# Seven-product units in the second half of the down-projections of a two-layer encoder, and wide turns at the borders

## The chip, the cores and the metric

One core of one Trainium2 chip. The metric is the device time of one execution in microseconds (us), the median of several runs; times inside it come from one profiled execution. Five engines run beside each other: TensorE (PE: matmuls, and PEld: loads of their weights), VectorE (DVE), ScalarE (ACT), GpSimd (POOL) and SyncE (SP, which issues most of the DMAs).

## The reference

A trunk of two encoder layers over 256 positions of width 2048, in float32. Layer 0 mixes tokens with grouped-query attention, layer 1 with dilated sliding-window attention. Behind each mixer stands a gated MLP:

```python
def conv_ffn(h, w_up, conv_w, conv_b, w_down):
    u = h @ w_up                                   # 2048 -> 2 * 5632
    u = depthwise_conv_width_3_over_positions(u, conv_w) + conv_b
    gate, val = jnp.split(u, 2, axis=-1)
    return (jax.nn.silu(gate) * val) @ w_down      # 5632 -> 2048

for i in range(2):
    hn = rms_norm(h, mix_norm[i])
    h = h + (mixer_a(hn, ...) if i == 0 else mixer_b(hn, ...))
    h = h + conv_ffn(rms_norm(h, ffn_norm[i]), w_up[i], conv_w[i], conv_b[i], w_down[i])
return rms_norm(h, final_norm)
```

## The kernel before

The 256 positions are two row blocks m of 128, and the residual `h` stays on the chip. A matmul of float32 precision is made of three: each operand is split into a high part (a copy by ACT in a shorter format) and a low part (the difference, by DVE), and high x high, high x low and low x high are added up in PSUM. Weights come in chunks of 512 rows (`kg`, four k-tiles) by 512 columns (`n`), as two raw tiles of 128x1024. `feed` (L106) handles one chunk: it loads the two raw tiles, has ACT make `wh` (L136) and DVE `wl` (L137) from each, and issues 24 matmuls: 4 k-tiles, 2 row blocks, 3 products (L124 to L126). `wh` and `wl` have four buffers each (`NHL`). The splits are issued under `high_priority` with an offset of `AHEAD` = 60: the scheduler may place them up to 60 instructions ahead of other work of their engine.

The MLP (`ffn`) goes through the 5632 hidden columns in two halves of 6 and 5 blocks of 512. In each half the up-projection makes a gate block and a value block in turn; `value_gen`, `gate_gen` and `flush` are generators that turn them, convolve them, multiply them and split the product for the down-projection (`act_split`). `step()` runs one piece of a generator between matmuls: those in `pending` in order, those in `beside` with `step(True)`. Then the half's down-projection adds its chunks into the residual, column block by column block (n = 0 to 3). Each column block has two PSUM accumulators, one for each row block; there are four accumulators (`new_acc`) and four other PSUM tiles (`ps_tile`).

In the first half two of the six chunks, 2 and 3, go through **seven-product units**. For a pair of column blocks, `fast_unit` (L496) treats the chunk as a 2x2 by 2x2 block product (blocks: pairs of k-tiles by row blocks on the left, pairs of k-tiles by column blocks on the right) and does it with 7 block products in place of 8: 42 matmuls in place of 48. It needs four sums of weights by DVE (L513), into the tiles `u`, and seven splits (ACT L514, DVE L515). The sums on the left are made once by `combined` (L479), when the chunk's product is split. Products 2, 4, 3 and 8 go straight into the four accumulators of the two column blocks, products 1, 5, 6 and 7 into the four other PSUM tiles. `fold` (L526) adds those into `h` afterwards: one copy by ACT, eight instructions by DVE. `pair` (L550) runs a list of (chunk, side): side 0 or 1 is a plain feed for one of the two column blocks, side None is a unit. Before the first unit it runs all generators to their end. The first half's list is: chunks 0 and 1 for both sides, unit 2, chunk 4 for both, unit 3, chunk 5 for both. The second half has no unit: `project2` (L193) handles columns 0 and 1 with the last chunk of both kept for the end, `project` columns 2 and 3, each with five chunks. In the last layer `project_last` handles columns 3 and the final norm.

`done` adds an accumulator to `h` (`add_residual`, L340) and, where a column block is final, sums squares (ACT) and starts `late_transpose` (L282). That one turns a quarter of `h` (a column block) for the next up-projection: for n < 3 with 16 block transposes on DVE (`block_T`, L275, recorded at L277), for n = 3 with two wide transposes (`quad_T`, L268) and moves of 32-row blocks on POOL, ACT and DVE. `out_proj` (L720) does the same behind the mixers.

Of the kernel before, what the change touches and what calls it, by code (L numbers as in the profile page):

```python
# [30 lines left out]
def tile_encoder(ctx: ExitStack, tc: tile.TileContext, x, xT, w_a, w_ao, q_gain, k_gain, w_b, w_bo,  # L31
# [249 lines left out]

    def late_transpose(hT, n, g, pool, tag):  # L282
        def put(kt, src):
# [4 lines left out]
        if n < 3:  # L288
            t = pool.tile([P, 4, NT], F32, tag=tag, name=nm("tT"), bufs=1)
            for b in range(4):  # L290
                yield
                for gr in range(4):
                    block_T(t, h[:, :, n * 512:(n + 1) * 512], b, gr)
            yield
            for j in range(4):
                put(4 * n + j, t[:, j, :])
            return
# [73 lines left out]
    def ffn(l, hT, ss_in, cw, g_next, last, side=None):  # L371
        with tc.tile_pool(name=nm("fpool"), bufs=1) as fp:
# [90 lines left out]
            def act_split(value):  # L463
                slots, k0 = value[5:]
                cv = value[2]
                if k0 // 4 in fast:
                    slots[-1 - k0 // 4] = combined(cv, k0)
                    ready.add(k0 // 4)
                    yield
                    return  # L470
                for j in range(4):
                    hi, lo = slots[k0 + j]
                    tc.keep_in_program_order(nc.scalar.activation(hi, cv[:, j, :], AF.Copy))
                    nc.vector.tensor_tensor(lo, cv[:, j, :], hi.bitcast(F32), ALU.subtract)
                    if j == 1:
                        yield
                ready.add(k0 // 4)

            def combined(cv, k0):  # L479
# [12 lines left out]
                for q, i in ((5, 0), (6, 1), (7, 2), (3, 3)):  # L492
                    pick[q] = own[0][:, i], own[1][:, i]
                return pick

# [30 lines left out]
            def fold(acc, n0, n1):  # L526
# [3 lines left out]
                tt = nc.vector.tensor_tensor  # L530
                one, two = (fp.tile([P, 2, 512], F32, tag="quad", name=nm("fold"), bufs=2) for _ in range(2))
                a, v, w, c = one[:, 0], one[:, 1], two[:, 0], two[:, 1]
                nc.scalar.activation(a, acc[1], AF.Copy)
                yield
                tt(v, acc[6], a, ALU.subtract)
                yield
                tt(w, acc[7], v, ALU.add)
# [4 lines left out]
                tt(hs(0, n0), hs(0, n0), a, ALU.add)  # L542
                yield
                tt(hs(1, n0), hs(1, n0), w, ALU.subtract)
                yield
                tt(hs(0, n1), hs(0, n1), c, ALU.add)
                yield
                tt(hs(1, n1), hs(1, n1), v, ALU.add)

            def pair(wd, ns, lhs, order, done, hurry=False):  # L550
                (a3, a8), (a2, a4) = new_acc(), new_acc()
                acc, begun = {2: a2, 3: a3, 4: a4, 8: a8}, set()
                sides = [a2, a4], [a3, a8]
                fasts = [kg for kg, side in order if side is None]
                for i, (kg, side) in enumerate(order):
                    while kg not in ready:
                        step()
                    if side is None:
# [10 lines left out]
                        if kg == fasts[-1]:  # L569
                            beside.append(fold(acc, *ns))  # L570
                        continue
                    mine = ((2, 4), (3, 8))[side]
                    end = not any(s == side for _, s in order[i + 1:])
                    feed(sides[side], lhs, kg, wd[ns[side], kg], not begun.issuperset(mine), end,
# [5 lines left out]
                    if end:  # L580
                        done(sides[side], ns[side])

# [13 lines left out]
            for hf, (p0, p1) in enumerate(HALVES):  # L596
                slots = {}
                ready.clear()
                new_us()
                fast = (2, 3) if hf == 0 else ()  # L600
                last_value = None
# [21 lines left out]
                def done(accs, n):  # L623
# [12 lines left out]
                    if hf == 1:  # L636
                        sumsq_cols(ss, n, junk)
                        start(late_transpose(hTn, n, g_next, fp, "cg"))

# [64 lines left out]
                both = {kg: [(kg, 0), (kg, 1)] for kg in rest}  # L704
                if not fast:
                    done(project2(wd, 0, 1, slots, rest, 1, lambda a: done(a, 0)), 1)
                    for n in (2, 3):
                        if last and n == 3:
                            project_last(wd, n, slots, rest, first_out, last_out)
                        else:  # L710
                            done(project(wd, n, slots, rest), n)
                    continue
                f0, f1 = ([(kg, None)] for kg in fast)
                for ns in (0, 1), (2, 3):
                    pair(wd, ns, slots, both[0] + both[1] + f0 + both[4] + f1 + both[5], done, ns[0] == 0)
            assert not spare
            extra[0] = None
        return hTn, ss

    def out_proj(w, slots, kgs, late, g_next, junk, pool, tag, cuts=()):  # L720
        hTn, ss = {}, new_ss()

        def done(accs, n):
            add_residual(accs, n)
            sumsq_cols(ss, n, junk)
            start(late_transpose(hTn, n, g_next, pool, tag))

# [36 lines left out]
    def mixer_a():  # L764
        with tc.tile_pool(name="apool", bufs=1) as ap:
# [246 lines left out]
            for g in range(4):  # L1012
                start(attend(g, project(w_a, g, hT, kgs)))
            return *out_proj(w_ao, slots, kgs, 1, 1, junk, ap, "t2", (2,)), cw

# [23 lines left out]
    def mixer_b(hT, ss_in):  # L1039
        with tc.tile_pool(name="bpool", bufs=1) as bp:  # L1040
# [29 lines left out]
            for hf in range(2):  # L1070
# [156 lines left out]
                for g in range(3):  # L1227
                    accs = project(w_b, 6 * g + 4 + hf, hT, kgs)
                    vs[g] = evac_split(bp, accs, rstd, v12[:, g - 1] if g else None)
                    if g == 0:  # L1230
                        start(value_stage())
            return *out_proj(w_bo, slots, [0, 2, 4, 1, 3, 5], 3, 3, junk, bp, "vl"), cw

# [88 lines left out]
```

## Time and profile before

| | |
|---|---|
| median of 3 runs | 2249.04 us (2248.47 to 2250.51) |
| profiled execution | 2247.76 us, of which the span from first to last instruction is 2246.0 us |
| busy: PE, PEld | 2233.1 us, 1852.2 us |
| busy: DVE, ACT, POOL | 1686.5 us, 1259.0 us, 733.0 us |
| granted TensorE clock, mean over the span | 0.999 |

A matmul's recorded duration (0.39 us) is longer than the distance between two of them, since they are pipelined. What a piece of work costs PE is therefore read from stretches of time and the number of matmuls in them, not from the sum of durations. An engine's busy share over the span is a mean over stages that have different limits.

### The profile page before, as it was taken

How to read it: one execution, taken by the hardware profiler on the slowest of the kernel's cores; microseconds unless marked ns; L12 is line 12 of the kernel's file. 1: busy time of each engine (PE TensorE's matmuls, PEld its weight loads, DVE VectorE, ACT ScalarE, POOL GpSimd, SP SyncE). 2: the span in 40 equal slices, each digit the busy share in tenths (PEclk: the TensorE clock that was granted, in tenths of full speed). 3: DMA queues.
4: the chain of work that ended last, by engine and by line, in shares of the span. 5: the costliest groups of instructions: out<-in, count | busy, mean ns of one | idle time of the engine just before them, and what ended most of it. 6: DMA issues, size and time to landing. Idle time of an engine off the chain costs nothing.

```text
span 2246.0 us, 28619 instructions
## 1 busy us (share of the span) xinstructions
PE 2233.1 (99%) x10041; PEld 1852.2 (82%) x10041; DVE 1686.5 (75%) x2241; ACT 1259.0 (56%) x1747; POOL 733.0 (33%) x971
## 2 busy tenths in 40 slices
PE   9999999999999999999999999999999999999998
PEld 7888888888888888888888888888888888888887
DVE  6877967778876776878886877686777798676765
ACT  7675555666545656555454554445655655465653
POOL 2342055662006553010052007002756500256510
PEclk9999999999999999999999999999999999999999
DMA  8665666665665566565556555566656566666663
GB/s 303 192 215 186 210 192 200 190 194 188 198 207 194 192 195 193 189 196 195 186 192 193 179 188 174 179 203 210 193 186 201 187 205 204 189 196 194 209 196 132
DMA packets 126048, 439.56 MB, mean 196 GB/s; under 512 B 14280, under 2 KB 18120, under 8 KB 125904
## 3 DMA queue, kind: packets, MB, share of 16 engines
q1 hardware_dynamic: 123056, 429.05, 59.1%
q0 software_dynamic: 2560, 8.39, 1.5%
q8 instruction: 78, 1.28, 0.2%
q14 instruction: 66, 0.54, 0.1%
q10 hardware_dynamic: 288, 0.30, 0.0%
HBM read 432.34 MB, written 5.34 MB: 195 GB/s over the span
## 4 chain that ended last, share of the span: by engine, by line
PE 93%; DVE 3%; POOL 2%; issue 1%; ACT 1%; DMA 1%; SPq 0%; DVEq 0%; POOLq 0%; ACTq 0%
PE acc L125 29%; PE acc L126 29%; PE acc L124 29%; POOL wide L272 2%; PE ps L521 1%; DMA raw<-in_w_a_dram 1%; PE ps L522 1%; DVE wl L515 1%; PE ps L520 1%; DVE wl L137 1%; PE acc L521 0%; PE acc L522 0%; PE acc L520 0%; PE ps L234 0%; PE ps L233 0%
## 5 line engine op out<-in xcount | busy, mean ns | idle before, releaser
L137 DVE TENSOR_TENSOR wl<-raw,wh 128x1024 fp32r<-128x1024 f32 (+1 forms) x772 | 961.7, 1250 | 419.6 <-ACT wh L136 413.9
L136 ACT ACTIVATE wh<-raw 128x1024 fp32r<-128x1024 f32 (+1 forms) x772 | 807.8, 1050 | 721.4 <-PE acc L126 645.8
L124 PE MATMUL acc<-wh,xh 128*128 128x512 f32 x2176 | 848.8, 390 | 0.2 <-ACT wh L136 0.2
L125 PE MATMUL acc<-wl,xh 128*128 128x512 f32 x2176 | 848.1, 390 | 0.5 <-DVE wl L137 0.4
L126 PE MATMUL acc<-wh,xh 128*128 128x512 f32 x2176 | 847.7, 390 | 0.0
L432 POOL COPY u<-quad 32x256 f32<-32x256 f32 x672 | 473.3, 704 | 349.0 <-DVE quad L268 322.6
L125 PEld LDWEIGHTS acc<-wl,xh 128*128 128x128 f32 x2176 | 409.0, 188 | 85.0 <-DVE wl L137 2.0
L124 PEld LDWEIGHTS acc<-wh,xh 128*128 128x128 f32 x2176 | 409.3, 188 | 84.3 <-ACT wh L136 0.6
L126 PEld LDWEIGHTS acc<-wh,xh 128*128 128x128 f32 x2176 | 408.9, 188 | 84.8
L124 PE MATMUL acc<-wh,a 128*128 128x512 f32 x880 | 343.0, 390 | 0.0
L125 PE MATMUL acc<-wl,a 128*128 128x512 f32 x880 | 342.5, 389 | 0.0
L126 PE MATMUL acc<-wh,a 128*128 128x512 f32 x880 | 342.5, 389 | 0.0
L126 PEld LDWEIGHTS acc<-wh,a 128*128 128x128 f32 x880 | 165.1, 188 | 34.5 <-DVE a L219 0.2
L125 PEld LDWEIGHTS acc<-wl,a 128*128 128x128 f32 x880 | 165.2, 188 | 33.9
L124 PEld LDWEIGHTS acc<-wh,a 128*128 128x128 f32 x880 | 165.3, 188 | 33.8
L272 POOL COPY wide<-quad 32x256 f32<-32x256 f32 x165 | 107.2, 650 | 171.8 <-DVE quad L268 162.7
L402 POOL MEMSET u<- 128x4 f32 x12 | 1.0, 105 | 400.0 <-DVE wl L515 212.2
L368 ACT ACTIVATE stg<-acc,rstd 128x512 f32<-128x512 f32 x122 | 82.8, 684 | 32.8 <-PE acc L126 32.8
L449 POOL TENSOR_TENSOR cv<-cg,cv 128x1024 f32<-128x1024 f32 x18 | 58.2, 3233 | 108.9 <-DVE cv L419 103.6
L419 DVE SCALAR_TENSOR_TENSOR cg<-u,cw,cg 128x256 f32<-128x256 f32 x176 | 82.2, 510 | 4.5 <-ACT cg L411 4.5
L419 DVE SCALAR_TENSOR_TENSOR cv<-u,cw,cv 128x256 f32<-128x256 f32 x176 | 73.6, 477 | 2.8 <-ACT cv L411 2.8
L268 DVE STREAM_TRANSPOSE quad<-stg 128x512 f32<-128x512 f32 x88 | 59.0, 696 | 8.6 <-ACT stg L368 8.6
(219 smaller groups left out, 1514.7 us busy)
## 6 DMA issues: line engine op xcount, KB each, us to landing
raw<-in_w_up_dram SPq DMA_DIRECT2D x352, 512.0 KB, 4.6
raw<-in_w_down_dram SPq DMA_DIRECT2D x176, 512.0 KB, 4.5
raw<-in_w_b_dram SPq DMA_DIRECT2D x144, 512.0 KB, 4.4
raw<-in_w_bo_dram SPq DMA_DIRECT2D x48, 512.0 KB, 3.9
raw<-in_w_a_dram SPq DMA_DIRECT2D x40, 512.0 KB, 4.7
raw<-in_w_ao_dram SPq DMA_DIRECT2D x32, 512.0 KB, 4.2
raw<-in_w_a_dram SPq DMA_DIRECT2D x16, 256.0 KB, 5.7
there<-quad POOLq DMA_DIRECT2D x6, 512.0 KB, 3.3
```

The costliest lines, as they stand in the source:

```text
L124: nc.tensor.matmul(accs[m], xh, wh[:, j, :], start=st, stop=False)
L125: nc.tensor.matmul(accs[m], xh, wl[:, j, :], start=False, stop=False)
L126: nc.tensor.matmul(accs[m], xl, wh[:, j, :], start=False, stop=sp)
L136: nc.scalar.activation(wh[:, c], r[:, c], AF.Copy)
L137: nc.vector.tensor_tensor(wl[:, c], r[:, c], wh[:, c].bitcast(F32), ALU.subtract)
L268: nc.vector.transpose(quad[:, :, at, :], src.rearrange("p (x c t) -> p c x t", c=4, t=32))
L272: nc.gpsimd.tensor_copy(o[32 * c:32 * c + 32, :, 32 * q:32 * q + 32], quad[32 * q:32 * q + 32, c])
L368: nc.scalar.activation(o[:, m, :], accs[m], AF.Copy, scale=rstd[:, m:m + 1])
L419: nc.vector.scalar_tensor_tensor(cj, halves(flat[:, j, o:o + NT])[:, ::-1], tap(n, j, i), cj, ALU.mult, ALU.add)
L432: nc.gpsimd.tensor_copy(o, src)
L449: made.append(eng.tensor_tensor(cv, cg, cv, ALU.mult).ins)
L515: nc.vector.tensor_tensor(wl, r, wh.bitcast(F32), ALU.subtract)
```

## The change

1. The units of the first half handle chunks 1 and 2 in place of 2 and 3 (`fast = (1, 2)` in both halves), and the list becomes: chunks 0 and 3, unit 1, chunk 4, unit 2, chunk 5.
2. In the second half columns 0 and 1 go through `pair` with two units: chunks 0 and 3 for both sides, unit 1, chunk 4 for side 0, unit 2, chunk 4 for side 1. Columns 2 and 3 stay plain. So chunks 1 and 2 are kept in both forms: `combined` hands back its parts, and `plain_too` makes the one split that the plain form lacks (into a slot of its own) and records the plain k-tiles.
3. `pair` takes its accumulators in another order (those of side 0 first), a side ends where no later feed or unit adds to it, and in the second half `finish` runs the fold to its end before `done`.
4. `fold` uses the tiles `stg` and `st` and yields less often.
5. `late_transpose` turns the quarters n < 3 with two wide transposes and 16 block moves, in turn on POOL and ACT, four to a step; callers hand in the tile for it.

```diff
@@ -279,21 +279,32 @@
 
     next_space = [None]
 
-    def late_transpose(hT, n, g, pool, tag):
+    def quad_place(o, quad, i0, i1):
+        for i in range(i0, i1):
+            q, c = QC[i]
+            dst, src = o[32 * c:32 * c + 32, :, 32 * q:32 * q + 32], quad[32 * q:32 * q + 32, c]
+            if i % 2:
+                nc.scalar.activation(dst, src, AF.Copy)
+            else:
+                nc.gpsimd.tensor_copy(dst, src)
+
+    def late_transpose(hT, n, g, pool, tag, new_quad):
         def put(kt, src):
             hT[kt] = new_hT(kt)
             split_scaled(*hT[kt][:2], src, gain[:, g, kt:kt + 1])
 
         yield
         if n < 3:
-            t = pool.tile([P, 4, NT], F32, tag=tag, name=nm("tT"), bufs=1)
-            for b in range(4):
-                yield
-                for gr in range(4):
-                    block_T(t, h[:, :, n * 512:(n + 1) * 512], b, gr)
+            quad = new_quad()
+            for m in range(2):
+                quad_T(quad, slice(m, 8, 2), h[:, m, n * 512:(n + 1) * 512])
             yield
+            o = wide_tile(pool, tag)
+            for i in range(0, 16, 4):
+                quad_place(o, quad, i, i + 4)
+                yield
             for j in range(4):
-                put(4 * n + j, t[:, j, :])
+                put(4 * n + j, o[:, 2 * j:2 * j + 2].rearrange("p m c -> p (m c)"))
             return
         space, quad_tag, wide_tag = next_space[0]
         src = h[:, :, n * 512:(n + 1) * 512]
@@ -464,7 +475,9 @@
                 slots, k0 = value[5:]
                 cv = value[2]
                 if k0 // 4 in fast:
-                    slots[-1 - k0 // 4] = combined(cv, k0)
+                    slots[-1 - k0 // 4], *parts = combined(cv, k0)
+                    if hf == 1:
+                        plain_too(k0, 20 + 2 * fast.index(k0 // 4), *parts)
                     ready.add(k0 // 4)
                     yield
                     return
@@ -491,7 +504,15 @@
                 pick = {1: (hA[:, 0], lA[:, 0]), 2: (hA[:, 1], lA[:, 1]), 4: (hB, lB)}
                 for q, i in ((5, 0), (6, 1), (7, 2), (3, 3)):
                     pick[q] = own[0][:, i], own[1][:, i]
-                return pick
+                return pick, v, sx
+
+            def plain_too(k0, spot, v, sx):
+                c = pair_slot(spot, [P, 2, 2, P], F32R, "c")
+                split_in_order(c[:, 0], c[:, 1], v[:, 0, :, 1])
+                for kt in range(4):
+                    b, j = divmod(kt, 2)
+                    one = (sx[:, 4, j], sx[:, 5, j]) if b else (c[:, 0, j], c[:, 1, j])
+                    slots[k0 + kt] = (sx[:, b, j], one[0]), (sx[:, 2 + b, j], one[1])
 
             def fast_unit(acc, pick, wap0, wap1, begun, end):
                 def load(wap, i):
@@ -528,30 +549,33 @@
                     return h[:, m, n * 512:(n + 1) * 512]
 
                 tt = nc.vector.tensor_tensor
-                one, two = (fp.tile([P, 2, 512], F32, tag="quad", name=nm("fold"), bufs=2) for _ in range(2))
+                one, two = (fp.tile([P, 2, 512], F32, tag=t, name=nm("fold")) for t in ("stg", "st"))
                 a, v, w, c = one[:, 0], one[:, 1], two[:, 0], two[:, 1]
                 nc.scalar.activation(a, acc[1], AF.Copy)
                 yield
                 tt(v, acc[6], a, ALU.subtract)
-                yield
                 tt(w, acc[7], v, ALU.add)
                 yield
                 tt(c, acc[5], v, ALU.add)
                 tt(v, acc[5], w, ALU.add)
                 yield
                 tt(hs(0, n0), hs(0, n0), a, ALU.add)
-                yield
                 tt(hs(1, n0), hs(1, n0), w, ALU.subtract)
                 yield
                 tt(hs(0, n1), hs(0, n1), c, ALU.add)
-                yield
                 tt(hs(1, n1), hs(1, n1), v, ALU.add)
 
             def pair(wd, ns, lhs, order, done, hurry=False):
-                (a3, a8), (a2, a4) = new_acc(), new_acc()
+                (a2, a4), (a3, a8) = new_acc(), new_acc()
                 acc, begun = {2: a2, 3: a3, 4: a4, 8: a8}, set()
                 sides = [a2, a4], [a3, a8]
                 fasts = [kg for kg, side in order if side is None]
+
+                def finish(side):
+                    while beside and hf == 1:
+                        step(True)
+                    done(sides[side], ns[side])
+
                 for i, (kg, side) in enumerate(order):
                     while kg not in ready:
                         step()
@@ -568,9 +592,11 @@
                         fast_unit(acc, lhs[-1 - kg], wd[ns[0], kg], wd[ns[1], kg], begun, end)
                         if kg == fasts[-1]:
                             beside.append(fold(acc, *ns))
+                            if 0 not in later:
+                                finish(0)
                         continue
                     mine = ((2, 4), (3, 8))[side]
-                    end = not any(s == side for _, s in order[i + 1:])
+                    end = not any(s in (side, None) for _, s in order[i + 1:])
                     feed(sides[side], lhs, kg, wd[ns[side], kg], not begun.issuperset(mine), end,
                          begun=[m for m in range(2) if mine[m] in begun])
                     begun.update(mine)
@@ -578,7 +604,7 @@
                         if pending:
                             step()
                     if end:
-                        done(sides[side], ns[side])
+                        finish(side)
 
             def flush(value):
                 yield
@@ -597,7 +623,7 @@
                 slots = {}
                 ready.clear()
                 new_us()
-                fast = (2, 3) if hf == 0 else ()
+                fast = (1, 2)
                 last_value = None
                 for p in range(p0, p1):
                     k0 = 4 * (p - p0)
@@ -635,7 +661,7 @@
                     add_residual(accs, n)
                     if hf == 1:
                         sumsq_cols(ss, n, junk)
-                        start(late_transpose(hTn, n, g_next, fp, "cg"))
+                        start(late_transpose(hTn, n, g_next, fp, "cg", lambda: quad_tile(fp, "quad", 2)))
 
                 def square_into(hs, sc):
                     nc.vector.scalar_tensor_tensor(junk()[:, :hs.shape[-1]], hs, 1.0, hs, ALU.mult, ALU.mult,
@@ -702,28 +728,28 @@
                     load_fin()
                 rest = [kg for kg in range(np_) if kg not in fast]
                 both = {kg: [(kg, 0), (kg, 1)] for kg in rest}
-                if not fast:
-                    done(project2(wd, 0, 1, slots, rest, 1, lambda a: done(a, 0)), 1)
-                    for n in (2, 3):
-                        if last and n == 3:
-                            project_last(wd, n, slots, rest, first_out, last_out)
-                        else:
-                            done(project(wd, n, slots, rest), n)
+                f0, f1 = ([(kg, None)] for kg in fast)
+                if hf == 0:
+                    for ns in (0, 1), (2, 3):
+                        pair(wd, ns, slots, both[0] + both[3] + f0 + both[4] + f1 + both[5], done, ns[0] == 0)
                     continue
-                f0, f1 = ([(kg, None)] for kg in fast)
-                for ns in (0, 1), (2, 3):
-                    pair(wd, ns, slots, both[0] + both[1] + f0 + both[4] + f1 + both[5], done, ns[0] == 0)
+                pair(wd, (0, 1), slots, both[0] + both[3] + f0 + [(4, 0)] + f1 + [(4, 1)], done, True)
+                for n in (2, 3):
+                    if last and n == 3:
+                        project_last(wd, n, slots, list(range(np_)), first_out, last_out)
+                    else:
+                        done(project(wd, n, slots, list(range(np_))), n)
             assert not spare
             extra[0] = None
         return hTn, ss
 
-    def out_proj(w, slots, kgs, late, g_next, junk, pool, tag, cuts=()):
+    def out_proj(w, slots, kgs, late, g_next, junk, pool, tag, new_quad, cuts=()):
         hTn, ss = {}, new_ss()
 
         def done(accs, n):
             add_residual(accs, n)
             sumsq_cols(ss, n, junk)
-            start(late_transpose(hTn, n, g_next, pool, tag))
+            start(late_transpose(hTn, n, g_next, pool, tag, new_quad))
 
         done(project2(w, 0, 1, slots, kgs, late, lambda a: done(a, 0), None, cuts), 1)
         for n in (2, 3):
@@ -1011,7 +1037,8 @@
 
             for g in range(4):
                 start(attend(g, project(w_a, g, hT, kgs)))
-            return *out_proj(w_ao, slots, kgs, 1, 1, junk, ap, "t2", (2,)), cw
+            return *out_proj(w_ao, slots, kgs, 1, 1, junk, ap, "t2",
+                             lambda: pair_slot(16, [P, 4, 8, 32], name="quad"), (2,)), cw
 
     scr = dpool.tile([24, 1024], F32, name="scr")
 
@@ -1229,7 +1256,8 @@
                     vs[g] = evac_split(bp, accs, rstd, v12[:, g - 1] if g else None)
                     if g == 0:
                         start(value_stage())
-            return *out_proj(w_bo, slots, [0, 2, 4, 1, 3, 5], 3, 3, junk, bp, "vl"), cw
+            return *out_proj(w_bo, slots, [0, 2, 4, 1, 3, 5], 3, 3, junk, bp, "vl",
+                             lambda: quad_tile(bp, "stg", 2)), cw
 
     hT, ss, cw = mixer_a()
     hT, ss = ffn(0, hT, ss, cw, 2, False, bias_lines)
```

## The prediction

> **What bounds the kernel now.** I read the page first, then who waited for whom on TensorE, then stretches around the seven-product units that the kernel already has, and last VectorE's order inside them. Page, busy times and the chain that ended last:
>
> ```profile
> span 2246.0 us, 28619 instructions
> PE 2233.1 (99%) x10041; PEld 1852.2 (82%) x10041; DVE 1686.5 (75%) x2241; ACT 1259.0 (56%) x1747; POOL 733.0 (33%) x971
> PE 93%; DVE 3%; POOL 2%; issue 1%; ACT 1%; DMA 1%; SPq 0%; DVEq 0%; POOLq 0%; ACTq 0%
> ```
>
> TensorE (PE) is never free: 93% of the chain is its matmuls. A matmul that goes is therefore time that goes, as long as the engine that feeds it keeps up. VectorE (DVE) is at 75% over the span, but that is a mean over unlike stages. Who waited, TensorE alone:
>
> ```profile
> PE ps L234 <- DVE qTl L219: 1.9, 1, 1.9
> PE ps L521 <- DVE wl L515: 1.2, 2, 0.6
> PE acc L125 <- DVE wl L137: 0.4, 2, 0.2
> ```
>
> Hardly anything waits, but the second row is a wait inside the seven-product unit (L521 is in `fast_unit`), once in each layer. So I cut the first half's down-projection into stretches. Columns: stretch and length, then busy us and instructions of PE, weight load, DVE, ACT, POOL, the granted clock and the DMA share. The counts include one or two matmuls that run over an edge.
>
> ```profile
> 542.70:553.38 10.68, 10.08 (x44) 7.72 (x43) 10.61 (x13) 7.01 (x7) 0.00 (x0) 1.00 0.46 142
> 553.39:564.28 10.89, 10.89 (x50) 9.01 (x49) 9.20 (x9) 4.33 (x5) 0.00 (x0) 1.00 0.77 257
> 564.29:573.94 9.65, 9.65 (x44) 7.87 (x43) 9.44 (x9) 7.81 (x8) 0.00 (x0) 1.00 0.53 182
> 1806.77:1817.46 10.69, 10.07 (x44) 7.72 (x43) 10.62 (x13) 7.03 (x7) 0.00 (x0) 1.00 0.45 155
> ```
>
> The first row is the first unit of layer 0 (chunk 2), the second the plain chunk 4 for both column blocks (48 matmuls), the third the second unit (42 matmuls), the fourth layer 1's first unit. A plain chunk costs 10.89 us, a unit that is fed in time 9.65, and the first unit of a half 10.68: 1.03 us more, with DVE busy 10.61 of 10.68. The same in layer 1.
>
> **The change part by part.** Matmuls. Four units replace four plain pairs of chunks (chunks 1 and 2 for columns 0 and 1 in the second half, in two layers). Each takes 48 matmuls out and puts 42 in: 10.89 - 9.65 = 1.24 us, together 4.96 us. That is the whole gain on offer, 0.22%; about 0.2% (4.5 us) is what a measurement of this kernel can tell from no change.
>
> What a unit asks of VectorE. It has seven low parts (L515) and four sums (L513) of 128x1024, a plain chunk pair four low parts. DVE's order in the existing first unit of layer 0:
>
> ```profile
> 530.30 0.75 DVE L474 TENSOR_TENSOR a<-cv,a 128x256 fp32r<-128x256 f32 x2
> ...
> 547.09 1.22 DVE L515 TENSOR_TENSOR wl<-raw,wh 128x1024 fp32r<-128x1024 f32 x1
> 548.23 1.21 DVE L513 TENSOR_TENSOR u<-u,raw 128x1024 f32<-128x1024 f32 x1
> 549.36 2.51 DVE L515 TENSOR_TENSOR wl<-u,wh 128x1024 fp32r<-128x1024 f32 x2
> 551.79 3.49 DVE L137 TENSOR_TENSOR wl<-raw,wh 128x1024 fp32r<-128x1024 f32 x3
> 555.99 1.22 DVE L137 TENSOR_TENSOR wl<-raw,wh 128x1024 fp32r<-128x1024 f32 x1 [0.71 <-ACT wh L136]
> ```
>
> From 547.09 to 548.23 is 1.14 us, so one such instruction costs 1.14 back to back and a unit 11 x 1.14 = 12.5 us of DVE for 9.65 us of PE. A unit runs DVE into debt; the plain chunk behind it (4 x 1.14 = 4.6 us for 10.89) pays it off, and the last row shows that: at 555.99 DVE is so far ahead that it waits for a buffer. This alternation, unit, chunk for both columns, unit, chunk for both, is what holds the first half's later units at 9.65.
>
> The second half's new order is: chunk 0 and chunk 3 for both columns, unit 1, chunk 4 for column 0 only, unit 2, chunk 4 for column 1, then columns 2. Between the units there are 5.45 us of plain matmuls (half of 10.89) in place of 10.89, and behind the second one 5.45 us before columns 2 begin. Up to the end of the first unit the work on DVE is that of the first half: four plain feeds, the last block's convolution, its product and split. So I put the existing first unit's 1.03 us on the new one too: 2 x 1.03 = 2.06. If DVE's earlier idle time covers it, it is 0.
>
> Where columns 2 begin there is a new wait. The four PSUM accumulators are all taken; columns 2 get those of column 0, which `add_residual` (L340) has to read first, and `finish` puts the whole fold ahead of that: one copy on ACT and eight DVE instructions of 128x512. Their pace, from layer 0's existing fold:
>
> ```profile
> 576.40 0.68 DVE L537 TENSOR_TENSOR fold<-ps,fold 128x512 f32<-128x512 f32 x1
> 577.00 0.68 DVE L539 TENSOR_TENSOR fold<-ps,fold 128x512 f32<-128x512 f32 x1
> ```
>
> That is 0.60 us each, and the read of the accumulator another 0.68. On layer 0's clock from 551.79, where DVE has finished the first unit: chunk 4 column 0 takes 2 low parts, the second unit 11 instructions, chunk 4 column 1 takes 2, and columns 2's first low part 1, in sum 16 x 1.14 = 18.24, then 8 x 0.60 + 0.68 = 5.48: DVE is done at 575.51. PE, from 553.38: 5.45 + 9.65 + 5.45 = 20.55, so it wants the accumulator at 573.93. It waits 1.6 us. That is the lower bound, with DVE never idle. `feed` runs its splits ahead of other work (60 places), and if the second low part of columns 2 also passes the fold it is 1.14 more: 2.7 us. Nothing in the trace tells which, and I take 2.2 in the middle: 2 x 2.2 = 4.4. DMA does not add: the raw tiles of the second unit reuse those of the first one, whose last reader, the sum at 548.23, ends at 549.44, 9 us ahead of the second unit's first matmul. Behind the stalled matmul everything on PE's queue waits; ACT's high parts wait with it because their four buffers are not emptied.
>
> Bound from below: a DVE that keeps up makes both waits zero. From above: 1.03 + 2.7 in each layer, and the clock, below.
>
> The clock. The longest wait in the table above, 1.9 us in the attention of layer 0, is followed by this (same columns):
>
> ```profile
> 141.00:143.70 2.70, 0.96 (x6) 0.63 (x4) 2.70 (x4) 1.53 (x3) 1.42 (x1) 1.00 0.84 244
> 144.50:147.90 3.40, 3.40 (x12) 2.80 (x12) 1.97 (x4) 1.38 (x5) 0.00 (x0) 0.58 1.03 268
> 147.90:151.30 3.40, 3.40 (x19) 2.94 (x18) 2.25 (x4) 0.96 (x2) 1.04 (x1) 1.00 0.77 257
> ```
>
> After 1.9 us without a matmul the granted clock was 0.58 over the next 3.4 us: 3.4 x 0.42 = 1.4 us lost, 12 matmuls where the next such stretch has 19. The waits of 0.6 us inside the units left the clock at 1.00. My 2.2 us lies just at this point. The Trainium skill, page "TensorE: Matmul & The Clock Gate", section "Part 1: The HAM clock gate (the "warmup" mystery)", says that the clock falls to half after at least one idle window of about 3.4 us. By that a wait of 2.2 us would cost nothing more; the trace shows a fall after 1.9, so I go by the trace and give it a rival of its own.
>
> Readiness. Chunk 3 now stands second, 10.9 us after the up-projection's end, where it stood fourth. Its counterpart in the first half (chunk 4) was split by 530.30 + 0.75 = 531.05 (the row above); that half's down-projection began at 542.70 - 2 x 10.89 = 520.9, so the split was there after 10.1 us. It just fits, with the first two k-tiles earlier still; cost 0.
>
> Preparing the combined chunks (four subtractions, three splits, the extra split that keeps the plain form) costs DVE some 3 us a chunk more and lies in the up-projection. The border quarters: per quarter 16 block transposes go, two wide ones come, and 16 moves on ACT and POOL:
>
> ```profile
> L277 DVE STREAM_TRANSPOSE tT<-h 32x256 f32<-32x256 f32 x144 | 62.8, 436 | 2.7
> L268 DVE STREAM_TRANSPOSE quad<-h 128x512 f32<-128x512 f32 x6 | 3.9, 690 | 0.4 <-ACT junk L258 0.2
> L306 ACT ACTIVATE wide<-quad 32x256 f32<-32x256 f32 x18 | 7.5, 415 | 1.0 <-DVE tot L332 0.8
> L272 POOL COPY wide<-quad 32x256 f32<-32x256 f32 x165 | 107.2, 650 | 171.8 <-DVE quad L268 162.7 <-DVE tot L332 2.5
> ```
>
> DVE is relieved of 16 x 0.436 - 2 x 0.69 = 5.6 us, ACT gets 8 x 0.415 = 3.3, POOL 8 x 0.65 = 5.2. All nine quarters lie beside 21.8 us or more of matmuls of the next column block (a plain projection of four chunks is 4 x 10.89 / 2) that neither feed nor read them; the quarter of columns 2, the last to come, has that long before the border. Cost 0; were the cover gone, 1.4 + 5.2 us of turning would stand in the open at each of three borders. Nor does the relief help the wait at columns 2, since the first quarter is turned only behind that read. The first half keeps its order of work with other chunks in the units: 0.
>
> Sum: -4.96 + 2.06 + 4.4 = +1.5 us. Against the profiled execution (2247.76, of which 2246.0 is the span) that is 2249.3. The median of the runs shown is 2249.04, 1.28 above the profiled one, so I forecast 2250.5.
>
> **The rivals.** (a) VectorE keeps up in both places: -4.96, 2244.1. For it speaks the page's 75%; against it the 12.5 us a unit asks, and that first units do wait today. (b) The first unit's wait comes as now, but the wait at columns 2 does not, because the fold is spread well between the splits: -4.96 + 2.06 = -2.9, 2246.1. Against it: the sum 575.51 counts only what must be done, in any order. (c) Slower: the wait at columns 2 is at the long end, 2.7, and the clock drops behind it in both layers: -4.96 + 2 x (1.03 + 2.7 + 1.4) = +5.3, 2254.3. It decides from a wait of about 1.9 us on. (d) Chunk 3 comes late at its new second place: were its split 4 us behind its counterpart's, PE would wait some 3 us, of which DVE's debt gets back about half: +1.5 + 2 x 1.5 = +4.5, 2253.5. Against it the 10.1 us above. That the units are not made is no case: the lists of order say so plainly.
>
> **How the numbers follow.** Forecast 0.47, (a) 0.07, (b) 0.16, (c) 0.23, (d) 0.07. Range 2245.5 to 2256: it takes in (b) and (c) with some spread and leaves out (a) and longer waits than 2.7 us with the drop. Slower by over 4.5 us are (c), half of (d) and a tail of the forecast: 0.3. Faster by over 4.5 us is (a) alone: 0.07. The rest, 0.63, is within 0.2%.
>
> **What would show it.** TensorE's instructions fall by 24. Right: in each layer's second half a first unit near 10.7 us, a second near 9.65, and then a wait of PE for L340 on DVE at the first matmul of columns 2, with DVE busy without a gap before it. A granted clock near 0.58 behind it would be (c). No such wait, or DVE idle ahead of it, would prove the DVE sum wrong; a wait for the split of chunk 3 (L474) would be (d); new waits at the borders on POOL's or ACT's moves would mean that their cover fails.

## The result and the profile after

The change makes the kernel slower: 2254.14 us (median of 12 runs, 2251.6 to 2257.99) against 2248.91 for the kernel before (12 runs); ratio 1.0022, 95% interval 1.0014 to 1.0030, or 5.2 us. The profiled execution took 2254.35 us, its span 2252.6. The forecast was 2250.5, its range 2245.5 to 2256.

The page after, the lines that answer to those of before:

```profile
span 2252.6 us, 28696 instructions
PE 2232.8 (99%) x10017; PEld 1847.2 (82%) x10017; DVE 1689.8 (75%) x2175; ACT 1305.5 (58%) x1833; POOL 784.0 (35%) x1043
```

TensorE has its 24 matmuls less (10017 for 10041), and the span is 6.6 us longer. VectorE's busy time is what it was: the new units' 16 sums and 12 further low parts, the fold's and the preparation's work took up what the border quarters gave back. Its mean share of 75% tells nothing of what follows. Who waited, TensorE alone, longest total first:

```profile
PE acc L124 <- DVE h L654: 2.9, 1, 2.9
...
PE acc L124 <- ACT wh L136: 2.0, 3, 1.1
...
PE ps L542 <- DVE wl L536: 1.2, 2, 0.6
...
PE acc L541 <- ACT wh L535: 0.9, 2, 0.4
PE acc L124 <- DVE h L351: 0.7, 1, 0.7
```

The first and the last row are new: a matmul into an accumulator waits for a VectorE instruction that writes `h`. L351 is `add_residual` in layer 0, L654 the same addition in the last layer's `done`. The row for L542 is the old wait of the first half's first units, unchanged. The row for L541 is new and belongs to the second half's first units, and so do two of the three waits for ACT in the second row, 0.4 us each; the third, 1.1 us, lies where the kernel begins and costs nothing against before (its matmul starts at 8.54 us, there at 8.52).

The second half's units as stretches (columns as before: length, busy us and instructions of PE, PEld, DVE, ACT, POOL, clock, DMA): the first and the second of layer 0, and the first of layer 1. A first unit's stretch holds one plain matmul beside its 42, a second unit's two.

```profile
887.64:899.18 11.54, 10.67 (x45) 7.84 (x44) 10.34 (x12) 6.85 (x7) 0.00 (x0) 1.00 0.40 132
904.48:914.72 10.24, 10.24 (x46) 8.12 (x45) 10.24 (x11) 7.58 (x8) 0.00 (x0) 1.00 0.61 195
2152.88:2164.42 11.54, 10.67 (x45) 7.84 (x44) 10.34 (x12) 6.84 (x7) 0.00 (x0) 1.00 0.45 135
```

Less 0.23 us for each plain matmul and 9.65 for a unit that is fed in time, a first unit waits 1.66 us and a second 0.1. VectorE's order at the first one's end, layer 0:

```profile
894.19 1.22 DVE L534 TENSOR_TENSOR u<-u,raw 128x1024 f32<-128x1024 f32 x1
896.62 1.22 DVE L536 TENSOR_TENSOR wl<-u,wh 128x1024 fp32r<-128x1024 f32 x1 [1.21 <-ACT wh L535]
```

The last sum of weights (L534) is followed by 1.2 us in which VectorE does nothing: ACT first has to make the high part of that sum, and the last low part needs it.

Where columns 2 begin, VectorE's order in layer 0 and, behind the second line of dots, in layer 1:

```profile
916.55 0.69 DVE L556 TENSOR_TENSOR fold<-ps,fold 128x512 f32<-128x512 f32 x1
917.15 0.68 DVE L351 TENSOR_TENSOR h<-acc,h 128x512 f32<-128x512 f32 x1
...
921.35 0.69 DVE L351 TENSOR_TENSOR h<-acc,h 128x512 f32<-128x512 f32 x1
...
2178.42 3.49 DVE L137 TENSOR_TENSOR wl<-raw,wh 128x1024 fp32r<-128x1024 f32 x3
2181.82 0.68 DVE L556 TENSOR_TENSOR fold<-ps,fold 128x512 f32<-128x512 f32 x1
2182.42 1.22 DVE L137 TENSOR_TENSOR wl<-raw,wh 128x1024 fp32r<-128x1024 f32 x1
...
2187.15 1.28 DVE L654 TENSOR_TENSOR h<-acc,h 128x512 f32<-128x512 f32 x2
```

TensorE at the same two places:

```profile
921.05 0.39 PE L124 MATMUL acc<-wh,a 128*128 128x512 f32 x1
922.09 0.50 PE L124 MATMUL acc<-wh,a 128*128 128x512 f32 x1 [0.65 <-DVE h L351]
...
2184.72 0.39 PE L126 MATMUL acc<-wh,a 128*128 128x512 f32 x1
2187.99 0.47 PE L124 MATMUL acc<-wh,a 128*128 128x512 f32 x1 [2.87 <-DVE h L654]
```

In layer 0 the first accumulator is read at 917.15, early in the fold, and only the second, read at 921.35 behind the rest of it, is waited for: the next matmul starts 1.04 us later instead of 0.23, a loss of 0.8 us. In layer 1 a second low part of columns 2 runs within the fold (2182.42) and both accumulators are read at its end: 3.27 instead of 0.23, a loss of 3.0. Then the clock (same columns as the stretches above):

```profile
2185.00:2188.00 3.00, 0.13 (x2) 0.04 (x1) 3.00 (x6) 1.18 (x2) 0.00 (x0) 1.00 0.87 273
2188.90:2192.30 3.40, 3.40 (x10) 2.66 (x9) 3.00 (x4) 1.32 (x5) 3.40 (x2) 0.51 0.41 125
```

Behind the long wait TensorE was granted 0.51 over 3.4 us: 1.7 us more. Together: 2 x (1.66 + 0.1) + 0.8 + 3.0 + 1.7 = 9.0 us of waits against 4.96 us of matmuls saved, +4.1. The rest of the span's 6.6 us has three parts. The plain matmuls of chunks 1 and 2 in columns 2 and 3, which now read the parts that `combined` hands back, come more slowly. This stretch is those two chunks in columns 2 of layer 0, 48 matmuls and one over the edge:

```profile
926.09:937.26 11.17, 11.17 (x49) 9.02 (x48) 9.59 (x13) 10.91 (x23) 7.08 (x10) 1.00 0.67 206
```

A plain pair of chunks takes 10.89: 0.28 us more, at four places, 1.1 us. Why these matmuls are slower no run shows. Next, the kernel after is already 0.5 us behind at the first matmul of layer 0's `out_proj` (159.72 us for 159.21), ahead of the change's first new instruction. The last 0.9 us or so are delays of about 0.1 us behind each wait and still smaller ones.

### The profile page after: what moved, and what is told of

The parts are those of the page before. It is cut to its first block, busy times and chain, and to the rows that moved or that the text cites. A ratio compares the mean times of both kernels' runs of the same rounds, so it can differ in the third digit from the quotient of the medians.

```text
span 2252.6 us, 28696 instructions
## 1 busy us (share of the span) xinstructions
PE 2232.8 (99%) x10017; PEld 1847.2 (82%) x10017; DVE 1689.8 (75%) x2175; ACT 1305.5 (58%) x1833; POOL 784.0 (35%) x1043
## 4 chain that ended last, share of the span: by engine, by line
PE 89%; DVE 6%; POOL 2%; issue 2%; ACT 1%; DMA 1%; SPq 0%; DVEq 0%; POOLq 0%; ACTq 0%
PE acc L125 28%; PE acc L124 28%; PE acc L126 28%; POOL wide L272 2%; DVE wl L536 2%; DVE wl L137 1%; DVE u L534 1%; DMA raw<-in_w_a_dram 1%; PE ps L542 1%; PE ps L543 1%; PE ps L541 1%; ACT wh L136 0%; PE acc L542 0%; PE acc L543 0%; PE acc L541 0%
## 5 line engine op out<-in xcount | busy, mean ns | idle before, releaser
L137 DVE TENSOR_TENSOR wl<-raw,wh 128x1024 fp32r<-128x1024 f32 (+1 forms) x756 | 947.5, 1259 | 409.3 <-ACT wh L136 404.9
L136 ACT ACTIVATE wh<-raw 128x1024 fp32r<-128x1024 f32 (+1 forms) x756 | 791.3, 1050 | 684.7 <-PE acc L126 616.9
L443 POOL COPY u<-quad 32x256 f32<-32x256 f32 x672 | 481.7, 717 | 346.0 <-DVE quad L268 319.7
L124 PE MATMUL acc<-wh,a 128*128 128x512 f32 x752 | 293.9, 391 | 4.4 <-DVE h L654 2.9
L125 PE MATMUL acc<-wl,a 128*128 128x512 f32 x752 | 293.5, 390 | 0.0
L126 PE MATMUL acc<-wh,a 128*128 128x512 f32 x752 | 293.4, 390 | 0.0
L124 PEld LDWEIGHTS acc<-wh,a 128*128 128x128 f32 x752 | 141.7, 188 | 34.8 <-issue 3.3
L272 POOL COPY wide<-quad 32x256 f32<-32x256 f32 x165 | 107.2, 650 | 171.6 <-DVE quad L268 162.7
L126 PEld LDWEIGHTS acc<-wh,a 128*128 128x128 f32 x752 | 141.5, 188 | 29.8 <-DVE a L219 0.2
L125 PEld LDWEIGHTS acc<-wl,a 128*128 128x128 f32 x752 | 141.5, 188 | 29.0
L289 POOL COPY wide<-quad 32x256 f32<-32x256 f32 x72 | 40.9, 568 | 182.9 <-DVE quad L268 170.2
```

Of the source, the lines that this page charges most:

```text
L124: nc.tensor.matmul(accs[m], xh, wh[:, j, :], start=st, stop=False)
L125: nc.tensor.matmul(accs[m], xh, wl[:, j, :], start=False, stop=False)
L126: nc.tensor.matmul(accs[m], xl, wh[:, j, :], start=False, stop=sp)
L136: nc.scalar.activation(wh[:, c], r[:, c], AF.Copy)
L137: nc.vector.tensor_tensor(wl[:, c], r[:, c], wh[:, c].bitcast(F32), ALU.subtract)
L272: nc.gpsimd.tensor_copy(o[32 * c:32 * c + 32, :, 32 * q:32 * q + 32], quad[32 * q:32 * q + 32, c])
```

## The experiments

Theory 1 is the prediction's: VectorE falls into debt in the second half, and its order at two places, the first unit's end and the fold ahead of columns 2, decides what that costs. Theory 2 lays the loss on the border moves on ACT and POOL. The experiments were run in three sets, each on its own chip beside the kernel before, whose medians there were 2248.49, 2249.03 and 2249.54 us. The change was not run again in them, so comparisons with it go by the difference from before.

**Borders alone.** The kernel before with the change's `quad_place` and `late_transpose` (and the tiles handed to it), nothing else of the change.

> The kernel before with the new turning of the border quarters alone (two wide transposes, 16 block moves on POOL and ACT for the nine quarters n < 3); no further unit. Theory 1 (VectorE's debt in the second half is the whole loss): nothing, 2248.9 within 1 us, since every quarter lies beside 21 us or more of matmuls. Theory 2 (the moves on ACT and POOL hold up splits): at least 2 us of the 5.2 us that the change lost show here, 2251 or more, as waits of TensorE for ACT's high parts near the borders.

Measured: 2247.64 us, ratio 0.9998 (0.9989 to 1.0007). Nothing lost, where theory 2 asked for 2 us or more.

**Units alone.**

```diff
-            quad = new_quad()
-            for m in range(2):
-                quad_T(quad, slice(m, 8, 2), h[:, m, n * 512:(n + 1) * 512])
...
+            t = pool.tile([P, 4, NT], F32, tag=tag, name=nm("tT"), bufs=1)
+            for b in range(4):
+                yield
+                for gr in range(4):
+                    block_T(t, h[:, :, n * 512:(n + 1) * 512], b, gr)
```

> The change without the new turning: its units, orders and fold, but the border quarters turned by 16 block transposes on VectorE as before. Theory 1: like the change, 2254, or up to 2 us more, because VectorE, which is in debt where columns 2 begin, gets 5.6 us more a quarter there. Theory 2: less than the change by 2 us or more, 2252 or below.

Measured: 2258.12 us, ratio 1.0044 (1.0032 to 1.0057), some 9.6 us over before, 4.4 worse than the change; more than theory 1 expected, and the opposite of theory 2, which falls. VectorE in layer 0, behind the start of columns 2:

```profile
925.09 5.37 DVE L277 STREAM_TRANSPOSE tT<-h 32x256 f32<-32x256 f32 x12
930.50 0.69 DVE L340 TENSOR_TENSOR h<-acc,h 128x512 f32<-128x512 f32 x1
931.10 1.21 DVE L137 TENSOR_TENSOR wl<-raw,wh 128x1024 fp32r<-128x1024 f32 x1
```

Twelve block transposes, 5.4 us, stand ahead of the next low part, which TensorE gets 2.0 us late. The change's new borders cost nothing and keep the first quarter off an engine that is already late: they are worth several microseconds here, and nothing without the units.

**Accumulators first.**

```diff
-                    while beside and hf == 1:
-                        step(True)
-                    done(sides[side], ns[side])
+                    if hf == 1:
+                        release(sides[side], ns[side])   # h += accumulator, both row blocks
+                        while beside:
+                            step(True)
+                    done(sides[side], ns[side], hf == 1) # without that addition
```

> The change with one order turned round in the second half: an accumulator is added into h before the fold instead of after it (the same instructions, sums in another order). Theory 1: the wait at the first matmuls of columns 2 (0.8 us in layer 0; 3.0 us in layer 1 and 1.6 us behind it at the lower clock) goes, since the accumulators come free some 4 us earlier: 5.4 us less than the change, 2248.7. Rival (the debt only moves): VectorE still has the fold to do, and the wait shows up at the second weight tile of columns 2 instead: less than 2 us gained.

Measured: 2248.12 us, ratio 1.0002 (0.9993 to 1.0010); theory 1 had 2248.7. In its list of waits neither L351 nor the last layer's addition stands any more; those of the first units do:

```profile
...
PE acc L124 <- ACT wh L136: 1.9, 3, 1.0
...
PE ps L542 <- DVE wl L536: 1.2, 2, 0.6
PE acc L541 <- ACT wh L535: 0.9, 2, 0.4
PE acc L125 <- DVE wl L137: 0.8, 4, 0.2
...
```

One order turned round, with the same instructions, takes back the change's whole loss. So the greater part of it was not a lack of VectorE time but eight instructions in front of two; most of that is layer 1's wait of 3.0 us and the 1.7 us of clock behind it.

**The two last sums together.**

```diff
-                        if q in sums:
-                            nc.vector.tensor_tensor(*sums[q], ALU.add)
+                        for k in {5: (5,), 7: (7,), 6: (6, 4)}.get(q, ()):
+                            nc.vector.tensor_tensor(*sums[k], ALU.add)
```

> The change with the unit's last sum of weights issued next to the one before it, instead of behind the split in between. In the second half's first unit VectorE stands idle for 1.2 us after that sum, while ACT makes the high part from it, and TensorE waits 0.6 and 0.7 us for it. Theory 1 (VectorE is the bound there): that idle time goes, 1.2 us less in each layer, and up to as much again at columns 2, where VectorE comes as much earlier: 2.4 to 4.8 us less than the change, 2249.3 to 2251.7. Rival (ACT's order is the bound): unchanged, 2254.

Measured: 2251.17 us, ratio 1.0012 (1.0003 to 1.0021): 2.7 us over before, where the change is 5.2 over, and inside theory 1's 2249.3 to 2251.7. VectorE at the first unit's end, layer 0, without the pause:

```profile
892.53 1.22 DVE L534 TENSOR_TENSOR u<-u,raw 128x1024 f32<-128x1024 f32 x1
893.66 2.51 DVE L536 TENSOR_TENSOR wl<-u,wh 128x1024 fp32r<-128x1024 f32 x2
```

The high part is made on ACT while VectorE makes the low part before it.

**Both mends.** The two diffs above.

> The change with both mends: the accumulators are added into h before the fold, and the unit's last two sums of weights stand together. Theory 1: they act in two places (columns 2; the end of the first unit) and add up: 2.2 us less than with the first mend alone, 2245.9. Rival (both pay off the same debt of VectorE): no more than the better of the two, 2248.

Measured: 2248.16 us, before 2249.03, ratio 0.9996 (0.9987 to 1.0005). Better than the first mend by about 1 us and not by 2.2; within the intervals neither answer is excluded. The trace of layer 1 shows where a part went, VectorE and below it POOL:

```profile
2184.84 1.62 DVE L563 TENSOR_TENSOR h<-h,fold 128x512 f32<-128x512 f32 x1
...
2186.99 0.68 DVE L565 TENSOR_TENSOR h<-h,fold 128x512 f32<-128x512 f32 x1
2187.59 1.78 DVE L566 TENSOR_TENSOR h<-h,fold 128x512 f32<-128x512 f32 x1
```

```profile
2184.62 1.29 POOL L664 TENSOR_TENSOR h<-h,fin 128x512 f32<-128x512 f32 x1 [46.84 <-issue]
2187.35 1.46 POOL L664 TENSOR_TENSOR h<-h,fin 128x512 f32<-128x512 f32 x1 [1.44 <-ACT junk L663]
```

Two instructions that take 0.68 us elsewhere took 1.6 and 1.8: each began just after a multiplication by the final gain had begun on POOL, and ended some 0.5 us after it.

**The product on POOL**, with both mends and in the kernel before.

```diff
-                yield from product(value, nc.vector)
+                yield from product(value)                # the default engine is POOL
```

> Both mends, and the last block's product of gate and value on POOL (3.2 us) instead of VectorE (1.14 us back to back) in every half. Theory 1: VectorE's debt ahead of each first unit shrinks by 1.1 us, which is more than the 0.55 to 0.8 us that TensorE still waits there: some 2.7 us less than with the mends alone, 2243.2. Rival: VectorE's queue stands still behind the split that waits for the slower product, and nothing or less than nothing is gained, 2246 or more.

> The kernel before with that product on POOL alone. Theory 1: only the first half's first unit has a wait to lose, 0.8 to 1.0 us in each layer: 1.6 to 2.0 us less than before, 2246.6. Rival as with the mends: 2248.5 or more.

Measured: 2257.26 us, ratio 1.0039 (1.0026 to 1.0052), and 2251.97 us, ratio 1.0013 (1.0004 to 1.0022). Both slower. In the first half the reason is one that no expectation named. The kernel before with that edit, VectorE and then POOL in the first half of layer 0:

```profile
537.28 1.22 DVE L515 TENSOR_TENSOR wl<-raw,wh 128x1024 fp32r<-128x1024 f32 x1
538.41 3.41 DVE L513 TENSOR_TENSOR u<-raw,raw 128x1024 f32<-128x1024 f32 x1
```

```profile
537.53 3.21 POOL L449 TENSOR_TENSOR cv<-cg,cv 128x1024 f32<-128x1024 f32 x1 [9.39 <-DVE cv L419]
```

A sum of 1.2 us took 3.4: it ended 1.1 us after POOL did. Taking 1.14 us of work away from VectorE cost it 2.2 us of standing still. In the second half of the kernel with the mends the rival comes true, here in layer 0: the product on POOL takes 5.49 us there (the last section shows it), ACT's split waits for it, and VectorE's queue stands 2.75 us behind that split:

```profile
892.03 1.10 DVE L487 TENSOR_TENSOR a<-cv,a 128x256 fp32r<-128x256 f32 x3 [2.75 <-ACT a L486]
```

**One unit.**

```diff
-                fast = (1, 2)
+                fast = (1, 2) if hf == 0 else (1,)
...
-                pair(..., both[0] + both[3] + f0 + [(4, 0)] + f1 + [(4, 1)], done, True)
+                pair(..., both[0] + both[2] + f0 + both[3] + both[4], done, True)
```

> The change with one unit (chunk 1) in the second half: chunks 0 and 2 for both sides, unit 1, chunks 3 and 4 for both. Gain on offer 2 x 1.24 us. Theory 1: the wait in the first unit stays (1.75 us a layer in the change), the wait at columns 2 goes, since two whole chunks of plain matmuls lie behind the unit: -2.5 + 3.5 = +1.0, 2249.5. Rival (preparing both forms costs by itself, or the order of the chunks does): well above, 2252 or more.

Measured: 2250.43 us, before 2249.03, ratio 1.0009 (1.0000 to 1.0018): +1.4 where +1.0 was expected. No wait at columns 2 is left (no row for L351 or the last layer's addition); the first unit's rows remain. A first unit eats its own gain: 1.66 us of wait against 1.24. The 24 plain matmuls that read the combined chunk's parts are slower here too, 5.58 us (925.20 to 930.78) for 5.45, four times, so keeping a chunk in both forms is not free.

**Fold behind the last chunk, split behind the first unit.** In the second half, with both mends, the fold and `done` of both columns come behind chunk 4 of column 1. The second kernel also delays the last chunk's split in the first half; the third is the kernel before with this delay alone.

```diff
+                    release(sides[side], ns[side])
+                    if side == 1:                        # nothing more at side 0
+                        while beside:
+                            step(True)
+                        for s in range(2):
+                            done(sides[s], ns[s], True)
...
-                            while pending or beside:
+                            while len(pending) > (hf == 0) or beside or not last_value[4]:
...
-                yield
-                yield
+                for _ in range(2 if hf else 18):
+                    yield
                 yield from act_split(value)
```

> Both mends, and in the second half the fold and the final handling of columns 0 and 1 come behind chunk 4 of column 1 instead of ahead of it (the accumulators are still added into h first). With the mends alone two of the fold's VectorE instructions took 1.6 and 1.8 us instead of 0.7 in layer 1, while POOL multiplied h by the final gain, and TensorE waited 0.85 us for a low part of columns 2 queued behind them; in layer 0 it waited 0.2 us. Theory 1: both waits go, 1 us less than with the mends, 2247.2. Rival: POOL's multiplications meet the low parts instead, and nothing is gained, 2248.2.

> The one before, and in the first half the split of the last chunk (four high parts on ACT, four low parts on VectorE, 1.35 us of it) is not run to its end ahead of the first unit, but between the matmuls behind it; that chunk is needed 30 us later. Theory 1 (VectorE's debt ahead of the first unit): the first unit's 1.0 us of wait goes in both layers, 2 us less than with the fold spread alone, 2245.2. Rival (the wait hangs on one chain through the unit's sums, not on the amount of work): unchanged, 2247.2.

> The kernel before with that later split in its first half alone. Theory 1: 2 us less than before, 2246.9. Rival: 2248.9, unchanged.

Measured, before 2249.54: 2246.61 us, ratio 0.9989 (0.9980 to 0.9998); 2245.45 us, 0.9984 (0.9975 to 0.9993); 2247.12 us, 0.9990 (0.9981 to 0.9999). The first and third edits gain about what was expected; the second kernel, 4.1 us under before and some 8.5 under the change (0.9984 against 1.0022), beats both. Of those 4.1 us the delay alone gives 2.4 (the third kernel), so the second half's units with every mend are worth 1.7 us (2245.45 against 2247.12; the intervals overlap) of the 4.96 on offer. The two traces say the same: from first to last matmul, the second half's down-projection takes 107.8 us for 108.6 in layer 0 and 105.0 for 105.9 in layer 1. The waits of the second kernel, TensorE alone, whole:

```profile
PE ps L234 <- DVE qTl L219: 2.2, 2, 2.0
PE ps L339 <- DVE warm L336: 1.5, 1, 1.5
PE ps L542 <- DVE wl L536: 0.8, 2, 0.4
PE ps L1042 <- ACT pr L961: 0.6, 1, 0.6
PE acc L125 <- DVE wl L137: 0.2, 1, 0.2
```

And the first half's first unit, as a stretch, 9.92 us where it was 10.68:

```profile
543.65:553.57 9.92, 9.92 (x44) 7.81 (x43) 9.88 (x9) 7.44 (x7) 0.00 (x0) 1.00 0.52 175
```

## Why the prediction was nearly right

**The matmuls** went as worked out, 24 of them, and a second unit comes to about 0.1 us from the 9.65 that the 4.96 us rest on. But the whole gain was never measured: the best kernel gets 1.7 us out of the units. Part of what is missing is a term that the prediction put at nothing without naming it: chunks 1 and 2 in plain form, at 11.17 us for 10.89, 1.1 us in all.

**The first unit.** Put at 1.03 us a layer, it waited 1.66. The kind was right (TensorE waits for the splits of the unit's last product), the cause only half. The prediction counted VectorE's work; what was added is a pause of 1.2 us in that work, since the scheduler put the last sum behind a split. Moving the sum took the pause away. By the prediction's own sign, "DVE idle ahead of it", its sum for VectorE was thus incomplete. That the amount of work matters too is shown by the later split of the last chunk: 1.35 us of VectorE less ahead of the unit, 0.76 us less of unit.

**The wait at columns 2** was forecast in its place, with its cause, and the kernel with the accumulators first shows it by turning one order round. Its size was wrong in both layers: 2.2 us forecast, 0.8 and 3.0 measured. "That is the lower bound" is the step that failed for layer 0: it let all eight instructions of the fold go ahead of both additions, but the scheduler read the first accumulator in the midst of them, so that TensorE could begin columns 2 with it. In layer 1 the order was the one called possible, with a second low part ahead (2.7 forecast).

**The clock.** Rival (c), a long wait and then a lower clock, happened in layer 1 alone, at 1.7 us where 1.4 was put; in layer 0 a wait of 0.8 us left it at full speed. The 1.4 was read from a stretch that begins 0.6 us after the clock had fallen. Taken from its fall, the same place in the kernel before loses 1.7 us too; the second row is that place in the kernel with one unit:

```profile
143.93:147.34 3.41, 3.41 (x10) 2.93 (x11) 2.40 (x4) 0.81 (x3) 0.00 (x0) 0.50 0.96 247
...
144.10:147.50 3.40, 3.38 (x17) 2.88 (x18) 2.46 (x4) 0.74 (x3) 0.00 (x0) 1.00 1.00 253
```

The wait ahead of both is the same 1.93 us, and behind the second the clock stayed at 1.00. So "It decides from a wait of about 1.9 us on" is too firm: at about 1.9 us the clock falls in some profiles and not in others. The result, +5.2 us, lies near (c)'s +5.3 by chance: it is the sum of one layer like (c) and one like a mild forecast, with 0.6 us a layer more in the first units and 1.1 us of slower plain matmuls. The Trainium skill's rule (page "TensorE: Matmul & The Clock Gate", Part 1), an idle window of about 3.4 us, would allow no loss behind a wait of 3.0; this trace shows one.

**Readiness and borders** at zero were right: no wait for L487, the split of chunk 3, appears, and the borders alone measured nothing. That "the relief [does not] help the wait at columns 2" was right of that wait and wrong of the stage: with block transposes a later low part of columns 2 comes 2.0 us late in layer 0, and the kernel loses 4 us more.

## What to carry to other kernels

A saving on the busiest engine is worth what the engine that feeds it can spare in that very stage; a mean share of 75% hid a stretch in which VectorE had none, and of 4.96 us on offer 1.7 came in at best. There, order counts more than amount: look for the few instructions that give a buffer back and put them ahead of those that only finish a result, and put a producer's last link early enough that the next engine's part of the chain is hidden. Before moving work to an idle engine, look whether the two can run side by side at all.

## What the runs showed of the hardware

A VectorE instruction with two inputs in SBUF took longer by about the time that a two-input POOL instruction beside it still had to run: 3.41 us for 1.22, ending 1.1 us behind POOL's end; 1.62 and 1.78 for 0.68 beside POOL's multiplications. The other way round it was POOL that was longer: its product, with VectorE busy, took 5.49 us in the second half of the kernel with both mends and the product on POOL, 3.21 in the first half of the kernel before with that edit.

```profile
886.05 5.49 POOL L460 TENSOR_TENSOR cv<-cg,cv 128x1024 f32<-128x1024 f32 x1 [10.42 <-DVE cv L430]
```

The Trainium skill, page "SBUF — State Buffer", section "Who interferes with whom", says that a VectorE instruction with two SBUF inputs contends with a GpSimd instruction that reads SBUF; section "🔬 SBUF: two separate sides" adds that whichever starts first holds the shared ports for its whole length and the other is blocked fully. The 3.41 us agree. That the first comes through whole is less clear: POOL's 3.21 us, begun during a low part of VectorE's (537.28 to 538.50), are no longer than its mean of 3.23 in the kernel before.

And the granted clock fell to 0.5 for 3.4 us behind the long wait at columns 2 in all three profiles that have it (2.7 to 2.9 us in the lists of waits: the change, the units alone, the two last sums together), and not behind 0.8. Behind the wait in layer 0's attention, 1.93 to 1.97 us in every one of the thirteen profiles, it fell in nine, the kernel before and the change among them, and stayed at 1.00 in four: the units alone, one unit, and the two with the product on POOL. What decides between them no run here shows.
